# A decoder step: weight sums made by transfers instead of additions, with negations, accumulations and the down products in another order

## The chip, the cores and the metric

The kernel runs on one core of one Trainium2 chip. The metric is device time in microseconds, the median of several runs. All durations below come from one profiled execution of the kernel before.

## The reference

One inference step of a two-layer decoder on 1104 rows (16 meta rows, 1024 prompt rows and 64 sample rows), width 1024, all in float32. Layer 0 mixes by mLSTM, layer 1 by attention with forget gates over a shared K/V and a paged cache. Behind each mixer stands the same feed-forward block:

```python
def swiglu(xn, w_gu, w_d):
    gu = xn @ w_gu
    return (jax.nn.silu(gu[..., :D_FF]) * gu[..., D_FF:]) @ w_d
...
        h = h + swiglu(rmsnorm(h, prm['norm_ffn'][l]), prm['w_gate_up'][l], prm['w_down'][l])
        if l == N_A_LAYERS - 1:
            shared = shared_kv(h, prm['norm_kv'], prm['w_kvf'], prm['b_fg_b'], prm['k_norm_b'])
```

The inner width D_FF is 2816. Outputs are the activations, the mLSTM state, and K, V and forget values.

## The kernel before

**Arithmetic.** A float32 operand is split into a high part (ACT, `whi` L367) and a low part (DVE, `wlo` L368); a product is three matmuls, high by high, high by low and low by high. The 1104 rows stand in three groups of 336, 384 and 384, feature by row.

**Stages, in order of time.** Loading and transposing the input, with the value projection behind it (0 to 133.5 us); query, key and the mLSTM (from 169.5); out projection and the start of the feed-forward block (to about 640); its units of two columns of blocks, some 21 us each (to about 1078); down (to about 1350); K, V and queries of layer 1 (to about 1715); attention; the second feed-forward block (2210 to 2725) and its down product (to 2976).

**Loading, L735 to 777.** Nine row tiles are transposed on PE (`hps`), and ACT and DVE copy each half into `hs` (L761, L764), one of two buffers; POOL makes a low part (`x0l`, L767), then stores `hs` to a DRAM copy of the residual, `hD` (L776).

**Gate/up.** It runs as a scheme of block products with fewer multiplications. POOL makes sums of weight blocks (L135), ACT and DVE split them, PE multiplies (`m`, L1566), DVE forms the results (L1514, L1515). Results go to DRAM tiles `hT` (L1522). Some are also needed negated: `h_minus` negates in place on ACT (L1538) and stores, all that have gathered at the end of every second unit. `ACCUMULATE` lists, unit by unit, sums of one `hT` tile into another by accumulating transfers on POOL's queue (L1543).

**Down.** It is 15 products (`DOWN`), in chains that share an accumulator, four 128-row blocks each; weights and operands are loaded a few steps ahead (`w_load`, `x_load`), split, and multiplied (`dps`, L1978). Accumulators lie in four banks of tag d, and DVE adds a finished chain into the residual `H` (L1960). Two products use a difference of weights, made by `w_sub` on POOL (L1705). Nine other weights are sums of blocks of `w_down`, read from DRAM tiles `wc`: `combine` makes them, in seven pieces per layer, by six loads (L2030), nine additions on DVE (L2035) and nine stores (L2036). Layer 0's pieces stand in the value projection, layer 1's in the projection of K and queries. The norm of the next stage runs on POOL among others (`ns`, L442).

**Order.** In gate/up and down the order of PE, DVE, ACT and POOL is as written (`manual_schedule`, `fixed`); elsewhere a scheduler orders an engine's instructions by their dependencies. Each engine then runs its list strictly in order; POOL's and SP's transfers wait in their engine's list too. POOL's transfers share one software queue; SP's, with the weight loads (L351, L101), a hardware queue.

Of the kernel before, what the change touches and what calls it, by code (L numbers as in the profile page):

```python
# [16 lines left out]
P = 128  # L17
# [41 lines left out]
PAIRS = ((2, 0, 0, 1), (12, 1, 0, 2), (7, 0, 1, 3), (9, 4, 3, 4))  # L59
# [6 lines left out]
LATER = (("s5", "n20"), ("s13", (2, 0)), ("s3", (2, 0)), ("s3", (2, 1)), ("s11", "n21"), ("s11", (2, 2)), ("s9", (2, 2)),  # L66
         ("s6", (2, 2)))
ACCUMULATE = {9: (("s1", (0, 1), 0, 4), ("s1", (0, 1), 4, 7)), 11: (("s5", (0, 2), 0, 4), ("s5", (0, 2), 4, 7)),
# [3 lines left out]
              19: tuple((a, b, 0, 4) for a, b in LATER[:4]), 20: tuple((a, b, 0, 4) for a, b in LATER[4:])}  # L72
DOWN = ((12, 1, ((1, 0, 1), (1, 1, -1)), None, True), (14, 1, ((0, 1, 1),), None, False),
# [203 lines left out]
class Net:  # L277
# [237 lines left out]
    def mlp(self, H, w, l, heads=None, cb=None, early=None):  # L515
# [8 lines left out]
        with self.pool(self.uid("nsp")) as sp, self.pool(self.uid("npp"), bufs=2, space=PSUM) as pn:  # L524
# [28 lines left out]
            with ExitStack() as c:  # L553
# [89 lines left out]
                order.enter_context(self.tc.manual_schedule(engines={E.PE, E.DVE, E.Activation}))  # L643

                rows = (4, 5, 6, 7, 0, 1, 2, 3) if cb else range(KT)
                for x, m in enumerate(rows):
# [14 lines left out]
            with cw if not cb else ExitStack():  # L661
# [8 lines left out]
                if cb:  # L670
# [3 lines left out]
                    self.ffn(H, flat, l, weights, order, mix, each, after, self.first_values, cw, cb, self.first_weights)  # L674
                else:
                    self.ffn(H, flat, l, weights, order, mix, each, None,
# [106 lines left out]
def phase_a(self, vt):  # L783
# [7 lines left out]
    with ExitStack() as c3:  # L791
# [13 lines left out]
        with ExitStack() as cw, self.pool("ppA0", bufs=4, space=PSUM) as pp:  # L805
# [21 lines left out]
            with self.pool("wcA") as wc:  # L827
                for c in range(3):
                    cols, evac = part(c)
                    for j in ((0, 1, 2), (3, 4), (5, 6))[c]:  # L830
                        self.combine(0, j, lambda x: wc.tile([P, 512], F32, name=self.uid("wc"), tag=f"wc{x}",
                                                             bufs=2 if isinstance(x, tuple) else 1))
                    self.tm_proj(cols, None, pp, "mm0", 4, evac, halves=None if c else ahead)
# [2188 lines left out]
```

## Time and profile before

| what | us |
|---|---|
| median of 3 runs (lowest to highest) | 2981.53 (2977.31 to 2983.31) |
| profiled execution | 2987.69 |
| its span | 2986.0 |
| PE busy | 2770.6 |
| DVE busy | 1898.1 |
| ACT busy | 1342.2 |
| POOL busy | 1175.1 |

The mean granted clock of TensorE was 0.973. The hardware queue moved 339.15 MB, the software queue 189.97 MB. Busy time is an average over the stages; a row "A <- B" in a view of waits says that A's engine was idle until B, with the total in us, how often, and the longest. L followed by a number is a line of the kernel before; rows of the changed kernel's order have its own line numbers.

### The profile page before, as it was taken

How to read it: one execution, taken by the hardware profiler on the slowest of the kernel's cores; microseconds unless marked ns; L12 is line 12 of the kernel's file. 1: busy time of each engine (PE TensorE's matmuls, PEld its weight loads, DVE VectorE, ACT ScalarE, POOL GpSimd, SP SyncE). 2: the span in 40 equal slices, each digit the busy share in tenths (PEclk: the TensorE clock that was granted, in tenths of full speed). 3: DMA queues.
4: the chain of work that ended last, by engine and by line, in shares of the span. 5: the costliest groups of instructions: out<-in, count | busy, mean ns of one | idle time of the engine just before them, and what ended most of it. 6: DMA issues, size and time to landing. Idle time of an engine off the chain costs nothing.

```text
span 2986.0 us, 53985 instructions
## 1 busy us (share of the span) xinstructions
PE 2770.6 (93%) x19981; PEld 2629.5 (88%) x19981; DVE 1898.1 (64%) x3781; ACT 1342.2 (45%) x2734; POOL 1175.1 (39%) x1714
## 2 busy tenths in 40 slices
PE   7769999999999889988988999999999999988998
PEld 7768888999999889988988988777899999988997
DVE  6453565787776656773366643577568777765676
ACT  5122354454444334443343444677544444433443
POOL 4522333156565510223476310455315556551031
PEclk9979999999999989998999999999999999999999
DMA  7855656223445699644577486544413344669973
GB/s 226 279 178 144 172 144 193 86 90 124 138 124 139 146 270 316 225 157 131 184 264 270 162 299 247 196 163 141 139 55 93 121 138 124 147 150 285 296 247 141
DMA packets 379683, 533.18 MB, mean 179 GB/s; under 512 B 36046, under 2 KB 282346, under 8 KB 378394
## 3 DMA queue, kind: packets, MB, share of 16 engines
q1 hardware_dynamic: 315730, 339.15, 35.0%
q0 software_dynamic: 62464, 189.97, 22.4%
q8 instruction: 157, 2.57, 0.4%
q14 instruction: 108, 0.88, 0.1%
q10 hardware_dynamic: 1224, 0.60, 0.1%
HBM read 373.32 MB, written 194.83 MB: 190 GB/s over the span
## 4 chain that ended last, share of the span: by engine, by line
PE 29%; DVE 6%; DMA 5%; issue 4%; POOL 4%; ACT 2%; SPq 0%; DVEq 0%; ACTq 0%; POOLq 0%
PE m L1566 8%; PE dps L1978 7%; PE sp L2784 2%; PE op L2880 1%; DMA hT<-Ht 1%; PE bps L293 1%; DVE s L2793 1%; PE tp L2843 1%; PE pops L293 1%; PE pops L294 1%; PE pops L295 1%; DVE slot L368 1%; PE bps L294 1%; PE bps L295 1%; PE ktp L2487 1%
## 5 line engine op out<-in xcount | busy, mean ns | idle before, releaser
L1566 PE MATMUL m<-x1h,slot 128*128 128x384 f32 x640 | 179.4, 339 | 3.8 <-DVE ns L1515 1.5
L368 DVE TENSOR_TENSOR slot<-slot,slot 128x512 fp32r<-128x512 f32 (+3 forms) x175 | 153.4, 878 | 46.2 <-ACT slot L367 39.2
L1978 PE MATMUL dps<-dn0xh,dn0wh 128*128 128x384 f32 (+1 forms) x444 | 152.0, 342 | 21.4 <-DVE vA L1960 14.4
L1566 PE MATMUL m<-x0h,slot 128*128 128x336 f32 x640 | 167.8, 317 | 0.0
L1978 PE MATMUL dps<-dn1xh,dn1wh 128*128 128x384 f32 (+1 forms) x444 | 150.6, 339 | 14.5 <-DVE Ht L1960 10.2
L367 ACT CAST slot<-slot 128x512 fp32r<-128x512 f32 (+3 forms) x175 | 114.3, 655 | 83.8 <-PE m L1566 65.7
L1978 PE MATMUL dps<-dn0xl,dn0wh 128*128 128x384 f32 (+1 forms) x444 | 150.2, 338 | 0.2 <-DVE dn0xl L368 0.2
L1978 PE MATMUL dps<-dn1xl,dn1wh 128*128 128x384 f32 (+1 forms) x444 | 149.7, 337 | 0.5 <-DVE dn1xl L368 0.5
L1978 PE MATMUL dps<-dn0xh,dn0wl 128*128 128x384 f32 (+1 forms) x444 | 150.0, 338 | 0.0
L1978 PE MATMUL dps<-dn1xh,dn1wl 128*128 128x384 f32 (+1 forms) x444 | 149.3, 336 | 0.0
L1566 PE MATMUL m<-x2h,slot 128*128 128x384 f32 x480 | 136.4, 338 | 0.0
L368 DVE TENSOR_TENSOR slot<-Ht,slot 128x256 fp32r<-128x256 f32 (+2 forms) x100 | 81.8, 820 | 78.2 <-ACT slot L367 78.2
L368 DVE TENSOR_TENSOR slot<-vA,slot 128x256 fp32r<-128x256 f32 (+2 forms) x100 | 81.5, 816 | 78.5 <-ACT slot L367 78.5
L135 POOL TENSOR_TENSOR slot<-vA 128x256 f32<-128x256 f32 x80 | 70.4, 889 | 153.2 <-DMA vA<-in_w_gate_up 131.5
L135 POOL TENSOR_TENSOR slot<-Ht 128x256 f32<-128x256 f32 x80 | 69.8, 883 | 153.2 <-DVE T_1l L168 69.8
L1566 PEld LDWEIGHTS m<-x1h,slot 128*128 128x128 f32 x640 | 117.6, 188 | 5.9 <-DVE ns L1515 2.1
L1566 PEld LDWEIGHTS m<-x0h,slot 128*128 128x128 f32 x640 | 113.9, 189 | 0.0
L442 POOL TENSOR_TENSOR ns<-ns,x2l 128x384 f32<-128x384 f32 (+1 forms) x18 | 24.5, 1360 | 225.6 <-ACT x2l L440 225.1
L1566 PE MATMUL m<-T_2h,slot 128*128 128x384 f32 x320 | 99.1, 351 | 13.8 <-ACT ns L1572 8.8
L1978 PEld LDWEIGHTS dps<-dn0xh,dn0wh 128*128 128x128 f32 x444 | 86.5, 195 | 24.7 <-ACT dn0wh L367 11.4
L1566 PE MATMUL m<-x1l,slot 128*128 128x384 f32 x320 | 108.0, 338 | 0.0
L1566 PE MATMUL m<-T_4h,slot 128*128 128x384 f32 x320 | 96.9, 343 | 9.8 <-ACT Ht L1572 4.4
(867 smaller groups left out, 10277.0 us busy)
## 6 DMA issues: line engine op xcount, KB each, us to landing
wraw<-in_w_in_a SPq DMA_DIRECT2D x40, 512.0 KB, 4.1
vA<-in_w_gate_up SPq DMA_DIRECT2D x40, 512.0 KB, 4.0
Ht<-in_w_gate_up SPq DMA_DIRECT2D x40, 512.0 KB, 4.2
kp<-in_cache_k SPq DMA_DIRECT2D x32, 512.0 KB, 6.9
vp<-in_cache_v SPq DMA_DIRECT2D x32, 512.0 KB, 8.4
wc<-wc POOLq DMA_DIRECT2D x63, 256.0 KB, 3.9
wc<-wcv POOLq DMA_DIRECT2D x63, 256.0 KB, 3.2
x2h<-wc SPq DMA_DIRECT2D x30, 512.0 KB, 10.1
```

What stands on the lines that cost most here:

```text
L135: self.net.nc.gpsimd.tensor_tensor(out=o, in0=a, in1=b, op=op)
L293: mm(ps, sh, mh, start=first, stop=False)
L294: mm(ps, sh, ml, start=False, stop=False)
L295: mm(ps, sl, mh, start=False, stop=last)
L367: self.nc.scalar.copy(hi, src)
L368: self.nc.vector.tensor_tensor(out=lo, in0=src, in1=hi.bitcast(F32), op=ALU.subtract)
L1566: nc.tensor.matmul(u.b[b][:, :n], w[p][:, k], x[q][:, k], start=new and k == i == 0, stop=k == 1 and i == 2, skip_group_check=True)
L1978: nc.tensor.matmul(acc[m][:, :c], w[a][:, k, m * P : m * P + P], x[b][:, k, :c], start=lead and k == q == 0, stop=k == len(ts) - 1 and q == 2,
L2487: nc.tensor.transpose(pk[:, j, :], R["kp"][n][:, (4 * g + j) * P : (4 * g + j + 1) * P], self.ident)
L2784: nc.tensor.matmul(ps[z][:, :n], a[r, qs], b[r, at : at + n], start=(y == 0), stop=(y == 2))
L2793: nc.vector.tensor_tensor_reduce(out=ss[z, u][:, at + o : at + e], in0=ps[z][:, o:e], in1=diag[x][:, z] if y else ncb[:, z, at + o : at + ...
L2843: nc.tensor.transpose(pt[:, h, y], ss[z, u][r, j * P : j * P + P], self.ident[r, r])
```

## The change

The sums of blocks of `w_down` are no longer made on DVE. `combine` is a generator of 18 steps per layer: a copy of a block from DRAM to DRAM into `wc`, or an accumulating transfer of a second block onto it, all on POOL's queue. The feed-forward block calls it in steps. Negations are split by quarters of a unit. `ACCUMULATE` and `LATER` are reordered so that consecutive transfers have different targets. The weight difference is made on DVE (`sub`). The chain of products 2, 8, 10, 5 comes first in down; accumulators lie in six banks; loads of the residual move. In layer 0 the down weights lie in the places of the gate/up weights, which stay open for the next stage. POOL joins the hand-written order from the last third of the out projection on.

```diff
-PAIRS = ((2, 0, 0, 1), (12, 1, 0, 2), (7, 0, 1, 3), (9, 4, 3, 4))
+COMBINED = ((2, (0, 0), None), (11, (0, 2), None), (12, (1, 0), None), (2, None, (0, 1)), (7, (0, 1), None),
+            (11, None, (1, 2)), (9, (0, 2), None), (8, 2, None), (12, None, (1, 2)), (13, 11, None), (8, None, (1, 1)),
+            (7, None, (1, 1)), (13, None, (1, 0)), (10, 8, None), (14, 13, None), (9, None, (1, 1)), (10, None, (1, 0)),
+            (14, None, (0, 0)))
...
-ACCUMULATE = {9: (("s1", (0, 1), 0, 4), ("s1", (0, 1), 4, 7)), 11: (("s5", (0, 2), 0, 4), ("s5", (0, 2), 4, 7)),
-              15: (("s8", (1, 0), 0, 4), ("s8", (1, 0), 4, 7), ("s6", (1, 0), 0, 4)),
+ACCUMULATE = {9: (("s1", (0, 1), 0, 4), ("s5", (0, 2), 0, 4)), 11: (("s1", (0, 1), 4, 7), ("s5", (0, 2), 4, 7)),
+              15: (("s8", (1, 0), 0, 4), ("s6", (1, 0), 0, 4), ("s8", (1, 0), 4, 7)),
...
-DOWN = ((12, 1, ((1, 0, 1), (1, 1, -1)), None, True), (14, 1, ((0, 1, 1),), None, False),
+DOWN = ((2, 1, ((0, 0, 1),), None, True), (8, -1, ((0, 2, -1),), None, False), (10, 1, ((1, 2, 1),), None, False),
+        (5, -1, ((1, 0, -1),), (1, 0), False),
+        (12, 1, ((1, 0, 1), (1, 1, -1)), None, True), (14, 1, ((0, 1, 1),), None, False),
         (1, -1, ((0, 0, -1),), (0, 0), False),
-        (2, 1, ((0, 0, 1),), None, True), (8, -1, ((0, 2, -1),), None, False), (10, 1, ((1, 2, 1),), None, False),
-        (5, -1, ((1, 0, -1),), (1, 0), False),
...
+                comb = self.combine(l)
...
+                    if x in (1, 5):
+                        next(comb)
...
-                    self.combine(0, j, lambda x: wc.tile([P, 512], F32, name=self.uid("wc"), tag=f"wc{x}",
...
-        def h_minus():
-            while negs:
-                o, x, j = negs.pop(0)
+        def h_minus(cs):
+            for y in [y for y in negs if y[0] in cs]:
+                negs.remove(y)
+                _, o, x, j = y
...
-                nc.gpsimd.tensor_tensor(out=a, in0=a, in1=b, op=ALU.subtract)
+                sub(a, a, b)
...
-                        if x % 2 == 0:
-                            h_minus()
+                    if x % 2 == 0 and g != 2:
+                        h_minus((("s1", "v2"), ("t4", "c15"), (), ("s2", "e"))[g])
+                    if g == 3:
+                        next(comb, None)
...
-            cw.close()
+            if not early:
+                cw.close()
...
+            if early:
+                view = lambda y: self.slots[y][:, : KT * P].rearrange("p (k n) -> p k n", k=2)
+                for x in range(2):
+                    got["raw", x] = view(x)
+                for x, y in ((0, 0), (1, 1), (2, 2), (4, 3)):
+                    got["wh", x], got["wl", x] = view(2 + y), view(LOW[y])
...
-                        acc[m] = bank("dps", "d")
+                        acc[m] = bank("dps", "f" if banks in (4, 5) or early and banks % 6 > 3 else "d")
+                        banks += 1
...
-                if 4 <= i < 12:
-                    h_add(*LATER[i - 4], 4, 7)
+                if i in (1, *range(4, 18, 2)):
+                    h_add(*LATER[i // 2 - (i > 1)], 4, 7)
...
+def combine(self, l):
+
+    e, w = self.nc.gpsimd, self.I["w_down"][l]
+    half = lambda z, k: w[7 * k * P : 7 * k * P + 7 * P, 512 * z : 512 * z + 512]
+    comb = self.comb[l] = {}
+    for p, a, b in COMBINED:
+        if a is not None:
+            comb[p] = self.dram.tile([7 * P, 512], F32, name=f"wc{l}_{p}")
+            e.dma_start(comb[p], half(*a) if isinstance(a, tuple) else comb[a])
+        else:
+            e.dma_start(comb[p], half(*b), accum_op=ALU.add)
+        yield
```

What this does to the lists of the engines is seen at three places. The first is POOL at the start of the program, in the loading of the input (`wc0_` and `wc1_` are the combined weights of layer 0 and 1; DMASW are the marks that earlier transfers of POOL's queue have landed). Before:

```order
L776 DMA hD_90<-hs_156 1024x1x80 [waits DVE_49,Activation_49]
L767 TENSOR_TENSOR x0l_3_146<-xy_223,x0h_2_145 128x4x128 [waits Activation_49]
L776 DMA hD_90<-hs_203 1024x1x128 [waits DVE_49]
L767 TENSOR_TENSOR x0l_3_146<-xy_284,x0h_2_145 128x4x128 [waits Activation_49]
L776 DMA hD_90<-hs_258 1024x1x128 [waits DVE_49]
```

And now:

```order
L2047 DMA wc0_12_6018<-in_w_down 896x512
L2047 DMA wc1_2_23912<-in_w_down 896x512
L2049 DMA wc0_2_5645<-in_w_down 896x512 [waits DMASW0_49]
L2047 DMA wc0_7_6162<-in_w_down 896x512
L782 DMA hD_90<-hs_156 1024x1x80 [waits DVE_49,Activation_49]
L2047 DMA wc1_11_24053<-in_w_down 896x512
L2047 DMA wc1_12_24284<-in_w_down 896x512
L2049 DMA wc1_2_23912<-in_w_down 896x512 [waits DMASW3_49,DMASW1_49]
L2047 DMA wc1_7_24428<-in_w_down 896x512 [waits DMASW2_49]
L773 TENSOR_TENSOR x0l_3_146<-xy_223,x0h_2_145 128x4x128 [waits Activation_49]
L782 DMA hD_90<-hs_203 1024x1x128 [waits DVE_49]
L773 TENSOR_TENSOR x0l_3_146<-xy_284,x0h_2_145 128x4x128 [waits Activation_49]
```

Two more copies, of `wc0_2` and `wc0_11`, stand a few rows earlier. The first five steps of both layers, ten transfers, now stand ahead of the second store of `hs`; no step of layer 0's feed-forward block or layer 1's holds them back. ACT's copies into `hs`, in the changed kernel, wait for the store two tiles earlier, through DMASW6 for the first store and DMASW3 for the second:

```order
L767 COPY hs<-hps_259 128x512 [waits DMASW6_49]
L771 CAST x0h_145<-xy 128x4x128 [waits DVE_49]
L817 COPY vA_101<-tmps_298 80x2x128 [waits PE_49]
L819 COPY gates<-tmps_298 80x16
L731 COPY rb<-rps_325 128x128 [waits PE_49]
L714 ACTIVATE vA_103,r_344<-xin 128x8x128 [waits DMAHW4_49]
L716 ACTIVATE r_344<-r_344,eps 128x1 [waits Activation_49]
L766 CAST x1h_329<-xy 128x4x128 [waits DVE_49]
L767 COPY hs<-hps_332 128x512 [waits DMASW3_49]
```

ACT's list itself has not moved here. The second place is SP, with the weight loads of query and key (`wraw`, 128x8x128). Before, they come after the loads of the cache's forget values and wait for transfers of POOL's queue, the stores of `combine`:

```order
L957 DMA lp<-in_cache_logf 128x16 [waits DMAHW5_49]
L351 DMA wraw_2233<-in_w_in_a 128x8x128 [waits DMASW5_49,DMASW4_49,DMASW6_49,DMASW3_49,DMASW7_49,DMASW0_49,DMAHW6_49,DVE_49,PE_49]
L351 DMA wraw_2310<-in_w_in_a 128x8x128 [waits DMASW6_49,DMASW2_49,DMAHW7_49,DMASW1_49,DMASW0_49]
L351 DMA wraw_2420<-in_w_in_a 128x8x128 [waits DMAHW6_49,DMAHW0_49,DVE_49]
L351 DMA wraw_2482<-in_w_in_a 128x8x128 [waits DMAHW7_49,DMAHW1_49,DVE_49]
```

And now:

```order
L354 DMA wraw_1264<-in_w_in_a 128x4x256 [waits DMAHW6_49,DMAHW4_49,DVE_49]
L354 DMA wraw_1996<-in_w_in_a 128x8x128 [waits DMAHW5_49,DMAHW2_49,PE_49]
L354 DMA wraw_1270<-in_w_in_a 128x4x256 [waits DMAHW0_49,DVE_49]
L354 DMA wraw_2073<-in_w_in_a 128x8x128 [waits DMAHW7_49,DMAHW1_49]
L354 DMA wraw_2183<-in_w_in_a 128x8x128 [waits DMAHW5_49,DVE_49]
```

They stand ahead of the forget values, between the last loads of the value projection, and wait for no transfer of POOL's queue. The third place is POOL in a late unit of layer 0's gate/up, with the accumulating transfers. Before:

```order
L1543 DMA hT_480_6101<-hT_487_6108 128x1344 [waits DMAHW6_49,DMAHW7_49,DMAHW5_49,DMASW0_49]
L1543 DMA hT_472_6093<-hT_477_6098 128x4x336 [waits DMAHW4_49,DMASW1_49]
L1543 DMA hT_473_6094<-hT_477_6098 128x4x336
L1543 DMA hT_473_6094<-hT_474_6095 128x1536 [waits DMAHW7_49,DMAHW1_49,DMASW2_49]
L135 TENSOR_TENSOR slot_5147<-vA_102 128x256 [waits DMAHW4_49,Pool_49]
```

And now:

```order
L1546 DMA hT_428_5872<-hT_431_5875 128x1344 [waits DMAHW6_49,DMAHW7_49,DMAHW5_49,DMASW6_49]
L1546 DMA hT_424_5868<-hT_419_5863 128x4x336 [waits DMAHW4_49,DMASW7_49]
L1546 DMA hT_423_5867<-hT_419_5863 128x4x336
L1546 DMA hT_427_5871<-hT_432_5876 128x1536 [waits DMAHW2_49,DMAHW1_49,DMASW1_49]
L138 TENSOR_TENSOR slot_4910<-vA_102 128x256 [waits DMAHW4_49,Pool_49]
```

Before, the fourth transfer adds into the tile that the third has just been given, and waits for it, with the weight sums (`slot`) behind; now its target is another. The negations of L1538 stand at the same places of ACT's list as before.

More of the change, by code (lines that the diff above doesn't have):

```diff
@@ L642, in mlp @@
                 fixed.close()
-                order.enter_context(self.tc.manual_schedule(engines={E.PE, E.DVE, E.Activation}))
+                order.enter_context(self.tc.manual_schedule(engines={E.PE, E.DVE, E.Activation, E.Pool}))
+                comb = self.combine(l)
                 rows = (4, 5, 6, 7, 0, 1, 2, 3) if cb else range(KT)
@@ L826, in phase_a @@
                     self.tm_proj(cols, None, pp, "mm0", 4, evac, halves=held, only=i)
[L827 to L830, printed above, removed]
-                        self.combine(0, j, lambda x: wc.tile([P, 512], F32, name=self.uid("wc"), tag=f"wc{x}",
-                                                             bufs=2 if isinstance(x, tuple) else 1))
-                    self.tm_proj(cols, None, pp, "mm0", 4, evac, halves=None if c else ahead)
+            for c in range(3):
+                cols, evac = part(c)
+                self.tm_proj(cols, None, pp, "mm0", 4, evac, halves=None if c else ahead)
         pp = c3.enter_context(self.pool("ppA", bufs=2, space=PSUM))
@@ L1484, in ffn @@
 @_add(Net)
-def ffn(self, H, flat, l, weights, order, mix, each, after, end, cw, cb=None, early=None):
+def ffn(self, H, flat, l, weights, order, mix, comb, each, after, end, cw, early=None):
     nc, I = self.nc, self.I
@@ L1792, in ffn @@
         ends = direct(1, 0)
+        next(comb)
         for i, k in enumerate(ks):
@@ L1804, in ffn @@
         ends = direct(0, 1)
+        next(comb)
         m.cast(2, pure(0))
@@ L1835, in ffn @@
         ends = direct(1, 1)
+        next(comb)
         weights.split(2, 0)
@@ L1914, in ffn @@
             self.sq = lambda x: x2[1].bitcast(F32)[:, x % 2 * SL : x % 2 * SL + SL]
-            ring = {"n": list(place["raw"]), "v": list(place["tmp"][:3])}
+            ring = {"n": place["raw"][:3], "v": place["tmp"][:3]}
+            if early:
+                ring = {"n": [got["raw", 2], got["tmp", 0]], "v": [got["tmp", 1], got["tmp", 2]]}
             def ny(nm):
@@ L2253, in then @@
                     behind.append(lambda: turn(q, v4))
-                if 4 * gi + c < 7:
-                    wide = [fp.tile([P, NT, 256], F32, name=self.uid("wcv"), tag="vst").rearrange("p i d -> p (i d)")
-                            for _ in range(2)]
-                    places = [y[:, z * 512 : z * 512 + 512] for y in wide for z in range(4)]
-                    self.combine(1, 4 * gi + c, lambda x: places.pop())
                 self.tm_proj([w[:, 256 * c : 256 * c + 256]], g, pp, "b", 4, evac, then)
```

51 lines of the change are left out of this document (18 added, 33 removed), and 4 rows, old and new, of the table ACCUMULATE.

## Prediction

> **What bounds the kernel now.** I read the page's first part, then PE's waits, then windows. In the page's totals:
>
> ```profile
> span 2986.0 us, 53985 instructions
> PE 2770.6 (93%) x19981; PEld 2629.5 (88%) x19981; DVE 1898.1 (64%) x3781; ACT 1342.2 (45%) x2734; POOL 1175.1 (39%) x1714
> ```
>
> TensorE bounds it, and the change neither adds nor removes a matmul. What can move is the 215 us in which PE is idle, and its clock after a gap. PE's waits name the holes:
>
> ```profile
> PE mmA L293 <- ACT whi L367: 35.8, 1, 35.8
> PE btp L2222 <- DVE raw L2249: 22.6, 11, 4.2
> PE dps L1978 <- DVE vA L1960: 14.4, 5, 6.7
> PE m L1566 <- ACT ns L1572: 10.6, 13, 2.4
> PE dps L1978 <- DVE Ht L1960: 10.2, 2, 5.9
> PE tmps L293 <- ACT slot L361: 7.6, 1, 7.6
> ```
>
> The largest is one wait of 35.8 us. The windows show each place (columns: window, length, then busy us and count for PE, PEld, DVE, ACT, POOL; clock, DMA share, GB/s):
>
> ```profile
> 10.00:20.00 10.00, 3.71 (x14) 2.38 (x15) 7.70 (x24) 7.39 (x15) 2.90 (x3) 1.00 1.08 373
> 60.00:133.50 73.50, 73.50 (x642) 73.37 (x640) 34.26 (x49) 13.89 (x32) 40.04 (x74) 1.00 0.85 278
> 133.50:169.50 36.00, 0.16 (x2) 0.05 (x1) 13.58 (x21) 1.72 (x3) 19.62 (x37) 0.54 0.78 265
> 650.00:800.00 150.00, 148.07 (x862) 146.34 (x863) 116.83 (x185) 72.95 (x152) 92.04 (x92) 1.00 0.35 108
> 834.00:860.00 26.00, 24.82 (x144) 24.13 (x144) 20.37 (x35) 11.72 (x26) 15.49 (x15) 1.00 0.70 182
> 1015.00:1050.00 35.00, 28.26 (x133) 26.43 (x132) 19.98 (x31) 9.83 (x22) 17.43 (x18) 0.85 0.75 149
> 1276.00:1292.00 16.00, 9.27 (x40) 8.91 (x39) 15.18 (x18) 5.92 (x9) 5.66 (x2) 0.79 0.79 275
> 1450.00:1500.00 50.00, 48.56 (x425) 48.24 (x424) 19.47 (x39) 17.44 (x46) 20.33 (x35) 1.00 0.59 199
> 1500.00:1650.00 150.00, 129.55 (x1058) 127.60 (x1057) 98.70 (x190) 55.74 (x158) 105.23 (x173) 0.95 0.80 275
> 2700.00:2750.00 50.00, 39.54 (x211) 38.60 (x211) 31.42 (x48) 19.25 (x28) 9.99 (x14) 0.90 0.93 304
> 2850.00:2900.00 50.00, 50.00 (x301) 49.87 (x301) 38.15 (x51) 22.44 (x33) 13.49 (x7) 1.00 0.76 261
> 2900.00:2950.00 50.00, 44.04 (x235) 43.04 (x234) 40.61 (x50) 19.70 (x28) 13.08 (x5) 0.90 0.61 211
> ```
>
> A stage's undisturbed rate comes from its best row: 862/150 = 5.75 matmuls per us in gate/up, 301/50 = 6.02 in down, 425/50 = 8.5 in the k/q projection. Missing matmuls over that rate are lost time.
>
> **Part 1, the start.** PE is full from 60 to 133.5, then stands until 169.5, because the query/key weights come late. SP says why, and ACT what it waits for:
>
> ```profile
> SPq L351 <- DMA wc<-wc: 50.1, 4, 22.9
> ACT whi L367 <- DMA wraw<-in_w_in_a: 44.4, 5, 34.1
> ```
>
> The weight load reuses memory of the combining, so it queues behind its last stores. In the changed order those loads stand before the log-forget loads and wait for no transfer of POOL's queue: the 36 us hole goes, if nothing else comes. But something does. The new order puts the first five transfers of both layers, eight copies and two accumulates of 896x512 floats (1.835 MB each), at the head of POOL's queue, ahead of hD<-hs. There are two hs buffers; ACT's copy into hs of row tile 2 waits for the first hD store to land, that of tile 3 for the second, and the second stands behind all ten. ACT runs in order, so everything for tiles 3 to 8 stands behind that copy. In the timeline before:
>
> ```profile
> 7.28 0.18 POOL L1016 TENSOR_SCALAR_AFFINE_SELECT bm<-bm 64x8 f32<-64x8 f32 x1
> 28.57 0.58 ACT L761 COPY hs<-hps 128x512 f32<-128x512 f32 x1
> 55.20 1.62 POOL L767 TENSOR_TENSOR x2l<-xy,x2h 128x512 fp32r<-128x512 f32 x1 [3.12 <-ACT x2h L765]
> ```
>
> From tile 3's copy to the last low half is 56.8 − 28.6 = 28.2 us, and from there to the end of the value projection 133.5 − 56.8 = 76.7 us of full PE. So query/key now starts at D + 28.2 + 76.7, where D is when the second hD store lands, or when it did before if D is early; before, at 169.5.
>
> D needs the price of the transfers. An accumulate has a row, in the window where one pair of hT sums ran, and the hardware loads of the first 60 us have another:
>
> ```profile
> q0 software_dynamic: 928, 1.20, 28.4%
> ...
> q1 hardware_dynamic: 6018, 8.26, 43.8%
> ```
>
> 28.4% of 26 us is 7.4 us of all 16 engines for 1.20 MB, so 1.835 MB takes 11.3 us. A DRAM-to-DRAM copy has no row: from below, the load rate at 10 to 20 us, 373 GB/s, gives 4.9 us; from above, the accumulate, which reads two operands, gives 11.3. I take 8, the middle, since a copy does more than a load and less than an accumulate. Half of the 8.26 MB of loads falls before D and shares the engines, 11 us, and the two hD stores (0.85 MB) take 2.3. Issue starts near 8 us (POOL's setup ends at 7.5). D = 8 + 8·8 + 2·11.3 + 13.3 = 108, query/key starts at 213: **+43 us**. With copies at 4.9 D is 83, +19; with accumulates at that rate also, D is 70, +6; with copies at 11.3, D is 134, +70. So the ends are +6 and +70.
>
> The Trainium skill, "DMA: Bandwidth & Descriptors", section "Latency and other measured facts", gives 214 GB/s as the full rate of copies between HBM tensors; by it a copy is estimated at 8.6 us and the sum would be −8 instead of −13. Its section "Issuing engines are not separate DMA queues" says that transfers issued from any engine run on the same 16 engines and interleave; by that the weight loads would suffer too, as counted here; the DMA share of 1.08 at 10 to 20 us agrees that there is no spare.
>
> **Part 2, combining leaves the k/q projection.** DVE's 63 additions per layer sit in its queue ahead of the normalisation that PE waits for:
>
> ```profile
> L2035 DVE TENSOR_TENSOR wc<-wc,wc 128x512 f32<-128x512 f32 x63 | 42.8, 691 | 54.4 <-DMA wc<-in_w_down 38.6 <-DMA wc<-wc 14.8
> ```
>
> Each is 0.69 us plus waits for its load. From 1500 to 1650 PE does 1058 matmuls against 8.5·150 = 1275: 25.5 us lost, of which the btp wait (22.6) is most. I take **−22**, bounds −10 (ACT or POOL, at 37% and 70% of that window, holds next) and −25.5.
>
> **Part 3, shared weight places.** The kvf loads no longer wait for a place of their own and stand eight rows earlier in SP's order: the 7.6 us slot wait shrinks, **−7**, bounds 0 and −10.
>
> **Part 4, what gate/up pays.** Thirteen transfers per layer are left, five copies and eight accumulates, 5·8 + 8·11.3 = 130 us of all engines, one per unit of about 21 us, over about 240 us. At 650 to 800 the DMA share is 0.35, so it becomes near 0.9. The weight loads' landing:
>
> ```profile
> vA<-in_w_gate_up SPq DMA_DIRECT2D x40, 512.0 KB, 4.0
> ...
> vA<-in_w_gate_up SPq DMA_DIRECT2D x3, 512.0 KB, 5.1
> ```
>
> 4.0 us over all, 5.1 in the window with accumulates, where PE lost only 26 − 144/5.75 = 1 us. The step is issued behind POOL's sums, when the next load goes out too, so they meet; the sums have some slack before the split. I take 1 us per accumulate step, **+16** for both layers; bounds 0 (slack covers it) and +70 (each of 26 steps delays a unit by 2.7 us). POOL's own issue, 1 to 2 us, hides in its waits for loads.
>
> **Part 5, same-target sums apart.**
>
> ```profile
> POOL hT L1543 <- DMA hT<-hT: 74.1, 7, 13.6
> POOL ns L442 <- ACT x2l L440: 225.1, 10, 56.8
> ```
>
> POOL stood 74 us for these; behind it stand the next unit's weight sums, then the split, then PE. From 1015 to 1050 PE made 133 of 201 matmuls: 11.8 us lost, with a clock of 0.85. ACT's negations wait there too (below), and stay. I take 8 of the 11.8 per layer: **−16**, bounds 0 and −24.
>
> ```profile
> ACT Ht L1538 <- DMA hT<-Ht: 36.3, 16, 5.0
> ACT vA L1538 <- DMA hT<-vA: 35.6, 15, 5.7
> ```
>
> The change splits the negations by quarter, but in ACT's order they stand where they stood before. I cost that edit at nothing; these 72 us of ACT waits, and what PE loses by them, remain.
>
> **Part 6, down.** The weight subtraction moves from POOL to DVE. It stood behind POOL's norm sums, which wait for ACT (the 225 us above):
>
> ```profile
> 2899.95 3.68 POOL L442 TENSOR_TENSOR ns<-ns,x2l 128x384 f32<-128x384 f32 x2
> 2903.59 3.39 POOL L1705 TENSOR_TENSOR x2h<-x2h,dn1raw 128x1024 f32<-128x1024 f32 x1
> ```
>
> PE loses (301 − 235)/6.02 = 11.0 us from 2900 to 2950, and at 1276 to 1292 (96 − 40)/6.02 = 9.3 us in layer 0. On DVE (81% busy in the late window) the 128x1024 operation costs 1 to 2 us, in reach of the row of 0.69 for 128x512; I count it inside the gain. Six accumulator banks shorten the waits for DVE's evictions (14.4 and 10.2 us) in part: 6 us in layer 0, 1 to 4 in layer 1, where the stage's start (2700 to 2750: 90 missing matmuls, 15 us) is bound by transfers at a share of 0.93 and stays. **−15** and **−12**; bounds −5 and −24, −3 and −25.
>
> **Sum.** 43 − 22 − 7 + 16 − 16 − 15 − 12 = −13 us. The profiled execution took 2987.69 us (1.7 around its span) and would take 2974.7; the runs' median is 2981.53, so I predict **2968 us**.
>
> **Rivals.** (a) *The hoisted transfers cost more* (slower): copies at the accumulate's rate. Place: the second hD store; price +70 instead of +43; sum +14, 2995 us. It decides from copies of 9.6 us on (13/8 over 8). For it: the start is full of loads, share 1.08; against: a copy reads one operand. 0.22. (b) *Gate/up starves* (slower): loads and steps start together and POOL's sums come late; 3 us per accumulate step are +48 instead of +16, 3000 us. For it: a share near 0.9; against: 1 us lost in 834 to 860. 0.14. (c) *The start is nearly hidden* (faster): all ten at the load rate, +6 instead of +43: 2931 us. For it: a copy's price may be a load's; against: the accumulate's row, and the loads already there. 0.20. (d) *It doesn't do what it says*: no pacing at the start, the negations unmoved, and if the reorderings merely move waits elsewhere, the 43 us of parts 5 and 6 shrink to 30: no change, 2981 us. 0.14. My forecast has 0.30.
>
> **Range and chances.** 0.2% (6 us) is about what a measurement of this kernel can tell from no change. Faster: forecast and (c), 0.50; same: (d), 0.14; slower: (a) and (b), 0.36. The likeliest case's own range is 2950 to 2975. All good ends together, 6 − 25.5 − 10 + 0 − 24 − 24 − 25 = −102.5, give 2879, which is not met at once; (c) with a little more of these is 2925. Upward, (a) and (b) together, 27 + 32 on 2968, give 3027.
>
> **What would show it.** Right: no wait of PE for whi near 133, but PE, ACT and POOL idle from about 25 to 108 us, ending with an hD store's landing, and query/key starting near 213; btp's wait for raw gone; no hT-to-hT wait on POOL around 1020 to 1050; norm sums no longer ahead of a weight subtraction. Wrong: query/key starting before 190 or after 235; weight loads in gate/up landing above 8 us and PE below 5.5 matmuls per us there; or in down new waits for transfers in place of those removed.

## The result and the profile after

The changed kernel takes 3045.18 us (median of 4 runs, 3042.38 to 3047.64) against 2979.49 us of the kernel before on the same chip: a ratio of 1.0219, 95% interval 1.0201 to 1.0236. It is 66 us slower where I forecast 13 us faster, outside my range of 2950 to 2975 us and beyond its far end of 3027. The page of the changed kernel:

```profile
span 3045.9 us, 53528 instructions
PE 2778.2 (91%) x19981; PEld 2632.6 (86%) x19981; DVE 1820.2 (60%) x3671; ACT 1341.2 (44%) x2734; POOL 1041.7 (34%) x1526
```

DVE and POOL have lost 78 and 133 us of work, and PE is about as busy as before. As the run is slower, that work did not bound it. PE's waits, the costliest:

```profile
PE hps L750 <- ACT hs L767: 51.1, 4, 28.6
PE m L1569 <- ACT Ht L1575: 20.7, 11, 5.4
PE m L1569 <- ACT fs L1575: 18.5, 8, 7.1
PE dps L2001 <- DVE vA L1982: 15.5, 4, 6.3
PE m L1569 <- ACT vA L1575: 15.2, 8, 5.0
```

The wait of 35.8 us for the query/key weights is gone and so is btp's for raw; a wait for ACT's copy into hs stands in their place, and gate/up (m, now L1569) waits longer for ACT's bank copies (the copies of results out of the accumulators): before, its four rows were 10.6, 9.4, 8.0 and 6.6 us.

Both kernels do the same matmuls in the same order, except inside down and for four small ones ahead of query/key, so the start of the same matmul in two traces shows how long each stage took. Five later kernels are in the same table (us). Each column is cut at the same matmuls, some of them a few us inside a stage: query/key's first matmul itself starts at 169.5 us before and at 195.9 after.

| stage | before | after | held | old comb. | moved | spread | attention |
|---|---|---|---|---|---|---|---|
| start to query/key | 173.1 | 198.1 | 134.7 | 175.0 | 136.6 | 136.3 | 137.1 |
| query/key, mLSTM | 323.6 | 318.5 | 321.2 | 320.4 | 354.9 | 319.5 | 318.7 |
| out projection, start of feed-forward | 153.9 | 154.3 | 167.9 | 155.2 | 155.6 | 165.2 | 161.3 |
| gate/up, layer 0 | 432.4 | 464.8 | 467.7 | 432.5 | 435.2 | 449.2 | 437.0 |
| down, layer 0 | 253.2 | 252.8 | 253.4 | 251.8 | 250.2 | 251.2 | 250.8 |
| transition, V | 139.2 | 125.9 | 125.9 | 125.9 | 127.0 | 133.9 | 132.6 |
| K and queries | 238.5 | 207.8 | 207.5 | 238.2 | 243.3 | 210.8 | 210.8 |
| sample attention, entry to prompt | 185.4 | 195.6 | 195.9 | 195.0 | 209.2 | 185.5 | 184.8 |
| prompt attention | 246.8 | 249.3 | 249.5 | 249.5 | 246.8 | 248.4 | 261.7 |
| out projection, layer 1 | 116.1 | 116.1 | 128.0 | 116.1 | 116.6 | 127.6 | 121.0 |
| gate/up, layer 1 | 455.2 | 493.8 | 492.6 | 456.8 | 458.7 | 460.3 | 457.7 |
| down, layer 1, end | 261.7 | 262.2 | 262.1 | 262.1 | 262.0 | 262.8 | 261.7 |

After against before: +25.0 at the start, −5.1, +0.4, **+32.4**, −0.4, −13.3, **−30.7**, +10.2, +2.5, 0, **+38.6**, +0.5: together +60, as the spans (3045.9 − 2986.0) say. The chain at the start is the one I had drawn. ACT stands idle until the stores of hs have landed, and its copies for row tiles 2 and 3 begin only at 65.8 and 92.3 us:

```profile
ACT hs L767 <- DMA hD<-hs: 48.9, 2, 25.9
```

```profile
65.75 0.59 ACT L767 COPY hs<-hps 128x512 f32<-128x512 f32 x1 [25.87 <-DMA hD<-hs]
92.28 0.59 ACT L767 COPY hs<-hps 128x512 f32<-128x512 f32 x1 [23.03 <-DMA hD<-hs]
```

In windows (the same columns as in the prediction) PE is nearly empty until then, with all transfer engines busy, and later full with the engines idle:

```profile
25.00:60.00 35.00, 4.62 (x19) 3.66 (x17) 4.14 (x13) 4.65 (x9) 5.52 (x6) 0.56 1.05 323
60.00:85.00 25.00, 5.78 (x33) 5.55 (x33) 3.75 (x12) 3.46 (x9) 2.09 (x2) 0.64 1.06 286
140.00:196.00 56.00, 56.00 (x491) 56.00 (x490) 2.45 (x2) 9.47 (x22) 0.00 (x0) 1.00 0.05 6
```

What the software queue and the loads moved in the first 100 us of the changed kernel (packets, MB, share of 16 engines):

```profile
q0 software_dynamic: 6097, 20.39, 68.1%
q1 hardware_dynamic: 4962, 7.21, 22.2%
```

The transfers themselves, in the page's list of issues of the changed kernel (KB each, median us to landing), with the weight loads of gate/up, whose medians were 4.0 and 4.2 us before:

```profile
wc<-in_w_down POOLq DMA_DIRECT2D x28, 1792.0 KB, 15.5
...
vA<-in_w_gate_up SPq DMA_DIRECT2D x40, 512.0 KB, 6.1
Ht<-in_w_gate_up SPq DMA_DIRECT2D x40, 512.0 KB, 5.1
...
wc<-wc POOLq DMA_DIRECT2D x8, 1792.0 KB, 7.9
```

Two of these medians need care. That of `wc<-in_w_down` mixes the ten transfers at the start, which queue one behind another, with those in gate/up. And the trace gives a landing for only 6 of the 40 vA loads and 14 of the 40 Ht loads: of the six, three land after 3.9 to 4.3 us, as before, and three after 7.9 to 10.0.

A copy from scratch to scratch lands after 7.9 us, which is 232 GB/s for 1.835 MB. The Trainium skill's figure for copies between HBM tensors ("DMA: Bandwidth & Descriptors", section "Latency and other measured facts", 214 GB/s at full rate, there with padded rows and on other queues) nearly agrees.

### The profile page after: what moved, and what is told of

Read it like the earlier page. It is cut to its first block, busy times and chain, and to the rows that moved or that the text cites. A ratio compares the mean times of both kernels' runs of the same rounds, so it can differ in the third digit from the quotient of the medians.

```text
span 3045.9 us, 53528 instructions
## 1 busy us (share of the span) xinstructions
PE 2778.2 (91%) x19981; PEld 2632.6 (86%) x19981; DVE 1820.2 (60%) x3671; ACT 1341.2 (44%) x2734; POOL 1041.7 (34%) x1526
## 5 line engine op out<-in xcount | busy, mean ns | idle before, releaser
L371 DVE TENSOR_TENSOR slot<-slot,slot 128x256 fp32r<-128x256 f32 (+2 forms) x193 | 176.6, 916 | 60.6 <-ACT slot L370 56.6
L2001 PE MATMUL dps<-dn0xh,slot 128*128 128x384 f32 (+1 forms) x704 | 187.4, 344 | 19.6 <-DVE vA L1982 15.5
L1569 PE MATMUL m<-x1h,slot 128*128 128x384 f32 x640 | 182.9, 343 | 18.3 <-DVE Ht L1516 6.5
L370 ACT CAST slot<-slot 128x256 fp32r<-128x256 f32 (+2 forms) x193 | 130.9, 681 | 94.8 <-PE m L1569 71.6
L1569 PE MATMUL m<-x0h,slot 128*128 128x336 f32 x640 | 168.4, 318 | 0.0
L2001 PEld LDWEIGHTS dps<-dn0xh,slot 128*128 128x128 f32 x704 | 132.0, 195 | 22.3 <-issue 14.0
L138 POOL TENSOR_TENSOR slot<-vA 128x256 f32<-128x256 f32 x80 | 74.1, 937 | 207.3 <-DMA vA<-in_w_gate_up 127.0
L1569 PEld LDWEIGHTS m<-x1h,slot 128*128 128x128 f32 x640 | 119.0, 190 | 22.4 <-DVE Ht L1516 7.1
L1569 PE MATMUL m<-T_4h,slot 128*128 128x384 f32 x320 | 100.9, 356 | 40.2 <-ACT Ht L1575 16.5
L1569 PE MATMUL m<-x2h,slot 128*128 128x384 f32 x480 | 135.8, 337 | 0.0
L2001 PE MATMUL dps<-dn0xl,slot 128*128 128x384 f32 (+1 forms) x352 | 120.6, 343 | 0.5 <-DVE dn0xl L371 0.5
L1569 PEld LDWEIGHTS m<-x0h,slot 128*128 128x128 f32 x640 | 114.4, 189 | 0.0
L1569 PE MATMUL m<-T_2h,slot 128*128 128x384 f32 x320 | 98.3, 348 | 15.9 <-ACT ns L1575 13.7
L1569 PE MATMUL m<-x1l,slot 128*128 128x384 f32 x320 | 108.9, 340 | 0.0
L1569 PEld LDWEIGHTS m<-T_4h,slot 128*128 128x128 f32 x320 | 61.1, 194 | 48.8 <-ACT Ht L1575 18.5
```

Source lines behind the costliest of these rows:

```text
L138: self.net.nc.gpsimd.tensor_tensor(out=o, in0=a, in1=b, op=op)
L370: self.nc.scalar.copy(hi, src)
L371: self.nc.vector.tensor_tensor(out=lo, in0=src, in1=hi.bitcast(F32), op=ALU.subtract)
L1569: nc.tensor.matmul(u.b[b][:, :n], w[p][:, k], x[q][:, k], start=new and k == i == 0, stop=k == 1 and i == 2, skip_group_check=True)
L2001: nc.tensor.matmul(acc[m][:, :c], w[a][:, k, m * P : m * P + P], x[b][:, k, :c], start=lead and k == q == 0, stop=k == len(ts) - 1 and q == 2,
```

## The experiments

**Held: the first five transfers of a layer kept at their written place.** They stood at the head of a hand-written order of POOL with no instruction and no data ahead of them; a small sum that reads the residual now stands there.

```diff
...
                     unit(2, m, x)
+                    if x == 0:
+                        nc.gpsimd.tensor_tensor(out=held, in0=H[2][:, m, :8], in1=H[2][:, m, 8:16], op=ALU.add)
```

> The changed kernel with one small addition on POOL, a sum of 8 columns of the residual, ahead of the first transfer of the combining in each layer, so that the first five transfers of a layer cannot run before the last third of its out projection. Theory A (the ten hoisted transfers hold the second store of the residual and with it ACT): the value projection ends near 133 us instead of 196, the 36 us wait for the query/key weights stays away, so query/key starts near 134; 56 us less than the changed kernel, about 2989 us, and up to 10 us more if the five transfers now disturb the out projection. Rival B (the input loads are slow for another reason, the order of the other loads): value projection still ends after 170 us, 3030 us or more.

3004.17 us (ratio to before 1.0067, interval 1.0041 to 1.0094), 41 us less than the changed kernel. Query/key starts at 134.7 us, 63 us earlier than in the changed kernel and 38 earlier than in the kernel before: theory A stands. What was too small is the price of five transfers at once beside the out projections: 13.6 us in layer 0 and 11.9 in layer 1, where up to 10 in all had been expected.

**Negations left out.**

```diff
-                nc.scalar.activation(o, o, AF.Copy, scale=-1.0)
                 h_put(o, x, j)
```

> The changed kernel without the negations: ACT no longer negates in place after the store, the positive values are stored twice, so that four of the stored operands have the wrong sign; everything else, the transfers of the combining too, is as in the changed kernel. Theory N (the transfers of the combining slow the stores of gate/up results, ACT waits for these landings before it negates, and the bank copies behind it keep PE waiting): the 32 us and 40 us which gate/up lost in layer 0 and 1 against the kernel before go, and some 20 us more of the waits that were there before; about 2960 to 2975 us. Rival L (the weight loads come late because they share the engines with the transfers): at most 15 us are gained, 3030 us.

3022.52 us (1.0141, 1.0114 to 1.0168), 23 us less: between the two. The stages decide. Gate/up takes 453.2 us in layer 0 and 482.0 in layer 1: 11.6 and 11.8 less than the changed kernel, but 20.8 and 26.8 more than the kernel before. Whether those 12 us per layer belong to the transfers, the same edit on the kernel before tells.

**Negations left out of the kernel before.** The edit is the same one.

> The kernel before without the negations (the positive values are stored twice, so four of the stored operands have the wrong sign); same-target sums in their old order. Theory N2 (PE's losses near the late units, 1015 to 1050 us and the like, come from ACT that waits for a store's landing before it negates in place, and not from POOL that waits for a same-target sum): gate/up becomes 10 to 20 us shorter in each layer though POOL's waits of 13 us stay; 2945 to 2965 us. Rival (my prediction's step, POOL's late weight sums): at most 3 us per layer, 2975 us or more.

2958.75 us (0.9928, 0.9899 to 0.9956), the time that theory N2 expects. Gate/up takes 420.8 and 445.2 us, 11.6 and 10.0 less than before. So the negations cost about 11 us per layer with and without the transfers, and the transfers cost 32.4 (453.2 − 420.8) and 36.8 us (482.0 − 445.2) without the negations, against 32.4 and 38.6 with them: theory N is out. The window that I had read as a loss by same-target sums, 1015 to 1050 us, in this kernel, first the window, then POOL's wait in it, with one wait longer than the one before:

```profile
1015.00:1050.00 35.00, 28.19 (x149) 27.55 (x148) 18.00 (x27) 11.37 (x25) 15.15 (x18) 0.90 0.72 150
...
POOL hT L1542 <- DMA hT<-hT: 21.6, 2, 14.9
```

The same wait before:

```profile
POOL hT L1543 <- DMA hT<-hT: 13.2, 1, 13.2
```

The stage as a whole is 11.6 us shorter with POOL waiting 21.6 us. The 149 matmuls, instead of 133, are not the same ones, since the program is 12 us further by then. By the starts of the same matmuls, those that took before 34.9 us, from 1015 to 1050, take 32.2 here: less than 3 of the 11.6 us come back in that window, the rest in other units. So theory N2 has the price of the negations right, but they explain only a small part of what PE loses in this window.

**The combining of the kernel before, all other edits kept.**

```diff
-                comb = self.combine(l)
+                comb = iter(())
...
+            with self.pool("wcA") as wc:
...
+                        self.combine(0, j, lambda x: wc.tile([P, 512], F32, name=self.uid("wc"), tag=f"wc{x}",
...
```

> The changed kernel with the combining of the kernel before (loads, additions on DVE and stores in the value projection and in the k/q projection) and all other edits. If the edits on same-target sums, down order, banks and the weight difference gain what I costed (16, 15, 12, and 7 for the shared places): about 2930 us. If they gain next to nothing, as the aligned traces of before and after suggest (gate/up in layer 0 from its unit 9 on 1 to 3 us less, down 0 and 0, the transition 14 less, attention 10 more): about 2973 us. In both cases the 36 us wait for the query/key weights is back and gate/up shows no loss.

2984.01 us (1.0005, 0.9994 to 1.0016): the other edits together gain nothing that can be measured, worse than either number. Gate/up and down are within 2 us of before, the transition is 13.3 us shorter, the entry to prompt attention about 10 us longer. So the 66 us, as a net sum of losses and gains, come with the combining by transfers. And the same-target wait: here POOL has none in that window, its sums begin at 1018 instead of 1033, and PE makes 144 matmuls instead of 133, but is later by 4 us at 1040 and level at 1050; ACT waits for the landings as before (before: `10.3, 3, 5.1`). The window, and ACT's wait in it:

```profile
1015.00:1050.00 35.00, 29.16 (x144) 28.08 (x143) 21.32 (x33) 10.71 (x24) 21.64 (x22) 0.85 0.81 171
...
ACT vA L1545 <- DMA hT<-vA: 11.2, 3, 5.0
```

**Accumulates replaced by copies.**

```diff
-            e.dma_start(comb[p], half(*b), accum_op=ALU.add)
+            e.dma_start(comb[p], half(*b))
```

> The changed kernel with each of the 18 accumulating transfers replaced by a plain copy of the same block onto the same place, so that the combined weights are wrong; as many transfers of the same size in the same order. Theory P (an accumulate holds the engines about twice as long as a copy, and that is what makes weight loads late): the start is 10 to 15 us shorter, the loss in gate/up falls by half or more, about 3000 us. Rival Q (the count of the transfers and their bytes decide, or their place in POOL's order): 3030 to 3045 us.

2973.16 us (0.9966, 0.9954 to 0.9977), 72 us less than the changed kernel, more than theory P had expected. Gate/up falls from 464.8 to 438.8 and from 493.8 to 463.0 us, of 32.4 and 38.6 lost 26.0 and 30.8 come back. In the start only 5.2 us do: two accumulates there are dearer than two copies by 2.6 us each. In this kernel's list of issues:

```profile
wc<-in_w_down POOLq DMA_DIRECT2D x28, 1792.0 KB, 10.1
...
vA<-in_w_gate_up SPq DMA_DIRECT2D x40, 512.0 KB, 4.2
```

In gate/up of layer 0 alone, where each goes by itself, POOL's queue (packets, MB, share of 16 engines) and its seven accumulates, in the changed kernel from 700 to 1110 us:

```profile
q0 software_dynamic: 12896, 32.30, 41.5%
...
wc<-in_w_down POOLq DMA_DIRECT2D x7, 1792.0 KB, 15.0
```

and the seven copies in their place in this kernel, from 690 to 1090 us:

```profile
q0 software_dynamic: 9968, 33.38, 34.9%
...
wc<-in_w_down POOLq DMA_DIRECT2D x7, 1792.0 KB, 9.4
```

An accumulate lands after 15.0 us and a copy after 9.4. The queue held the engines 170 us (41.5% of 410) instead of 140 (34.9% of 400), some 4.4 us more per accumulate. The few landings that the trace gives of the weight loads (6 of 40) have a median of 4.2 us with copies, 4.0 before and 6.1 with accumulates. Who waits for those loads are POOL's weight sums, here in layer 0's gate/up of this kernel:

```profile
POOL slot L138 <- DMA vA<-in_w_gate_up: 71.5, 11, 10.4
```

of the changed kernel:

```profile
POOL slot L138 <- DMA vA<-in_w_gate_up: 127.0, 14, 14.1
```

and of the kernel before:

```profile
POOL slot L135 <- DMA vA<-in_w_gate_up: 58.5, 12, 10.5
```

**The transfers moved out of gate/up**, into the value projection, query/key and output gates (layer 0) and the projection of K and queries (layer 1), each behind a small sum on POOL that reads a fresh result.

```diff
+def paced(self, l, at):
...
+    with self.tc.manual_schedule(engines={mybir.EngineType.Pool}):
+        self.nc.gpsimd.tensor_tensor(out=self.held, in0=at[:, :8], in1=at[:, 8:16], op=ALU.add)
+        next(comb, None)
```

> The changed kernel with the 18 transfers of the combining taken out of gate/up and spread one by one over other stages, each held back by a small sum on POOL that reads a result just made: layer 0's 7 over the value projection, 6 over query/key, 5 over the output gates; layer 1's 18 over the projection of K and queries, one for every fourth row tile. Theory A+L (the loss is where the transfers stand: ahead of the residual's stores at the start, and beside the weight loads of gate/up): from the aligned traces, the start 40 us less than before, the transition and k/q 13 and 31 less, attention 13 more, gate/up as in the kernel before, so about 2905 us, and up to 20 more if the transfers disturb their new neighbours. Rival M (such transfers slow whatever runs beside them, since the engines' time is the same everywhere): k/q and query/key lose what gate/up gains, above 2960 us.

3005.45 us (1.0079, 1.0055 to 1.0103): a miss of 100 us. The start and gate/up are as theory A+L says (136.6; 435.2 and 458.7), but query/key with the mLSTM takes 354.9 us, 36 more than in the changed kernel, K and queries 243.3, 35 more, sample attention 14 more. The seven in the value projection cost next to nothing: 136.6 against 134.7. PE's waits in this kernel from 130 to 500 us, for a load of what was stored on POOL's queue, and for the store's buffer, and the one in K and queries over the run:

```profile
PE sps L1280 <- DMA qk<-qkD: 12.5, 2, 10.5
PE mmA L296 <- ACT stg L878: 11.4, 2, 7.7
...
PE btp L2264 <- DVE raw L2291: 18.9, 7, 6.0
```

So rival M is right where the neighbours use POOL's own queue: the transfers into and out of qkD land after 6.4 us there (median, longest 16.6) instead of 4.5 (longest 8.8) in the changed kernel. Whether they are late by the queue's order or by the engines' time was not tried apart.

**The slot counter begun at 0** (on the moved kernel).

```diff
-                self.slot = 1
+                self.slot = 0
```

> The kernel with the transfers moved (first of this batch), and the counter of shared weight places begun at 0 instead of 1 after layer 0's down, so that SP's loads for prompt attention wait for the same transfers as in the kernel before and not for PE's last gate product. Theory S (the 11 us lost at the entry to prompt attention come from this place): 10 us less than the moved kernel, the entry takes 14 us and not 25. Rival: the transition loses its 13 us gain in exchange, no difference.

2999.36 us (1.0065, 1.0045 to 1.0085). The entry to prompt attention (80 matmuls at its start) falls from 24.7 to 13.9 us as theory S says, and the transition with V grows from 127.0 to 132.8, so about half of what the entry gains is lost there, where the rival expected all of it. The 6 us less in the medians is within what the intervals leave open; the stage times are plain. In the changed kernel SP's first load for prompt attention waits for PE's last gate product, with the other loads behind it, where the kernel before had four of them out at 1868 us:

```profile
SPq L2707 <- PE bps L298: 15.4, 1, 15.4
```

The counter decides which shared place the last weights lie in, and those places become the attention's.

**The weight difference back on POOL** (on the moved kernel).

```diff
-                sub(a, a, b)
+                nc.gpsimd.tensor_tensor(out=a, in0=a, in1=b, op=ALU.subtract)
```

> The kernel with the transfers moved (first of this batch), with the weight difference in down back on POOL. Theory D (the difference was late on POOL and is as late on DVE, whose splits and additions fill it at that point): down in both layers within 4 us of the moved kernel. Rival, my prediction's step (POOL's queue behind the norm sums costs 9 and 11 us): 15 to 20 us more than the moved kernel.

3007.4 us (1.0086, 1.0065 to 1.0108). Down takes 254.1 us instead of 250.2 in layer 0, and 265.0 instead of 262.0 with the end in layer 1: theory D, within 4 us; the move is worth 3 to 4 us per layer, not 9 to 11.

**Spread: placed where nobody waits.** Layer 0: 8 in the value projection, 5 in the out projection and the start of feed-forward, 5 in single units of gate/up; layer 1: 3 in V, 10 in prompt attention, 5 in the out projection; counter at 0.

```diff
...
+                    if groups.index((hp, g)) in (2, 5, 8, 11, 14, 17, 20, 23, 26, 29):
+                        self.step(1)
```

> The changed kernel with the 18 transfers per layer placed where the traces of the runs so far show neither loads that PE waits for nor traffic on POOL's queue that others wait for: layer 0's 8 over the value projection, 5 over the out projection and the start of feed-forward, 5 in every second or third unit of gate/up; layer 1's 3 in the value projection of K/V, 10 in prompt attention (one for every third group), 5 in its out projection; the slot counter as in the kernel with that one edit. Theory L (an accumulate is dear only beside a stream that somebody waits for): the start is 40 us shorter than in the kernel before, query/key as before, k/q 31 shorter, gate/up of layer 0 at most 12 longer, attention at most 10 longer: 2910 to 2940 us. Rival M (such transfers disturb whatever runs beside them): attention and the out projection lose 30 us or more, 2965 us or above.

2957.79 us (0.9921, 0.9899 to 0.9944): faster than both kernels, by less than theory L expected. Prompt attention takes its ten for nothing (248.4 against 249.3). The out projections lose 10.9 and 11.5 us, gate/up of layer 0 16.8 us for five steps. The out projection's wait in this kernel:

```profile
PE ghps L1488 <- DVE ogc L1490: 8.7, 1, 8.7
```

**All of layer 1 in prompt attention**, with the steps in another order, so that the value projection takes four of the accumulates.

```diff
...
+                    if groups.index((hp, g)) in (1, 3, 4, 6, 8, 10, 11, 13, 15, 16, 18, 20, 21, 23, 25, 27, 28, 30):
+                        self.step(1)
```

> The last placement with all 18 transfers of layer 1 in prompt attention, where 10 of them cost nothing, none in the K/V value projection and the out projection, and the steps of a layer in another order, so that layer 0's value projection takes four accumulates and four copies. Theory L: the out projection of layer 1 gives back its 11 us, gate/up of layer 0 3 to 6 us with fewer accumulates left, attention stays within 10 us: 2940 to 2950 us. Rival M (18 are too many for attention: its loads of keys and rows for the next heads come late): attention 20 us or more longer, 2965 us or above.

2944.38 us (0.9875, 0.9854 to 0.9896): the fastest of all, 39 us less than the kernel before on the same chip and about 100 less than the changed one. Gate/up of layer 0 gives back 12 us, but not by fewer accumulates, as expected: three accumulates and two copies stand there in both kernels, in another order, and the last two a unit earlier here. The out projection of layer 1 gives back 7; 5 of its loss stay, though no transfer stands there any more. Neither was followed up. Eighteen steps cost prompt attention 13 us, more than the 10 expected. PE there now waits for POOL, and POOL for a load of attention's own, which the ten steps of the kernel above did not delay:

```profile
PE tp L2915 <- POOL rx L2908: 10.7, 3, 4.9
```

```profile
POOL nd L2802 <- DMA ncb<-cD: 9.0, 2, 8.7
```

## Why the prediction was wrong

**Part 1, the start: mechanism right, size off.** The copies into hs, the second store behind ten transfers, the vanished hole: each is in the trace. D was sized at 108 us and the copy for tile 3 began at 92; the start costs +25.0 instead of +43. The term that was mis-sized is the price of the transfers. In the run with copies for accumulates the software queue's 20.90 MB of the first 100 us held the engines 61.1 us, which is about 5.4 us per copy where I had put 8; in the changed kernel 20.39 MB took 68.1 us, so an accumulate held them about 4 us longer, some 9.6 us where I had put 11.3. The loads went the other way: 22 us where I had put 11.

**Part 4, what gate/up pays: the step that failed.** I took 1 us per accumulate step from a window in which PE lost 1 us beside a pair of hT sums, 1.2 MB. Measured are +32.4 and +38.6 us, 71 instead of 16, or 4.4 us per accumulate step, just past its bound of 70. Rival (b) had the place right, late weight loads through shared engines, and priced it at 48. The runs show that the loss is the transfers': by the starts of the same matmuls it grows in layer 0 from nothing to 33.6 us while they go out, until about 932 us of the changed kernel, and not afterwards. Four fifths of it are the accumulates' own (26.0 and 30.8 us return with copies of the same size), 3.3 and 3.9 us on average for each beyond a copy's price, and POOL's sums then wait 127 us for the loads instead of 58.5 in layer 0. The engines were not as full there as I had summed: their share from 671 to 938 us, while the transfers went out, is 0.76, where I wrote near 0.9. Nor could the landings I compared carry the choice: 4.0 us rests on 6 of the 40 loads, and 5.1 on one of three. Why PE lost only 1 us beside the hT sums stays open. How the loads' lateness reaches PE I argue from the rows: POOL, then ACT's and DVE's splits, then ACT's bank copies; no run isolates it. The Trainium skill's sentence that transfers from any engine interleave on the same 16 engines ("DMA: Bandwidth & Descriptors", section "Issuing engines are not separate DMA queues") agrees with this, and so would have spoken for rival (b).

**Part 5, same-target sums: false.** The step "behind it stand the next unit's weight sums, then the split, then PE" did not hold. With POOL's wait gone (the old combining) gate/up is unchanged, and with POOL's wait longer (before without negations) it is 11.6 us shorter. ACT's wait for a landing before it negates in place, which I quoted and took as staying, costs PE more than POOL's wait; but it does not explain the window either. The 236 matmuls around it take 53.4 us before, 53.1 with the sums in the new order (the old combining), 50.0 without negations, and 47.8 with the new order and no negations (the changed kernel without negations). At the stage's best rate, 5.75 per us, they would take 41. What holds PE there for more than half of the lost time stays open.

**Part 6, down: false.** The weight difference, no longer behind POOL's norm sums, is now behind DVE's splits; ACT waits for DVE instead. The 18 us around the same place (DVE's is the third busy time of a window), and what ACT waits for, first before (ACT's row from 2660 to 2990 us), then after:

```profile
2898.00:2916.00 18.00, 13.71 (x79) 13.42 (x78) 17.71 (x14) 6.74 (x10) 14.30 (x6) 0.96 0.67 221
...
ACT dn1wh L367 <- POOL x2h L1705: 9.3, 4, 5.6
```

```profile
2960.00:2978.00 18.00, 14.41 (x81) 13.48 (x80) 17.28 (x21) 8.11 (x12) 3.28 (x2) 1.00 0.76 259
...
ACT dn1wh L370 <- DVE x2h L1517: 5.6, 2, 4.4
```

DVE was full in that stretch already, 17.7 of 18 us; I had read DVE's 81% over 50 us and not these 18. Whatever the six banks gain in layer 0, down as a whole is 0.4 us shorter there. One loss that stands against it lies at 1180 to 1193 us of the changed kernel, where its first chain is evicted (added to the residual): PE waits for DVE's eviction, DVE for ACT, ACT for an operand that is loaded while sums into hT still run:

```profile
PE dps L2001 <- DVE vA L1982: 6.3, 1, 6.3
...
ACT dn0xh L1744 <- DMA dn0tmp<-hT: 16.0, 2, 8.3
...
POOL hT L1546 <- DMA hT<-hT: 11.0, 2, 8.3
```

**Parts 2 and 3: right in kind.** K and queries gain 30.7 us against 22, more than my bound of 25.5; the transition gains 13.3 against 7, more than its bound of 10 as well. What I did not see is the other end of the shared places, +10.2 us at the entry to prompt attention.

**The sum.** Predicted 43 − 22 − 7 + 16 − 16 − 15 − 12; measured +25 − 31 − 13 + 71 + 0 + 0 + 0, and +10 at the entry, +2.5 in prompt attention and −5 in query/key, which I did not follow up. Two errors add up: a cost on a stage that PE bounds was taken at its light end, and three gains were booked from the engine that waited longest, not from what PE waited for. The start, smaller than forecast by 18 us, and the larger gains of parts 2 and 3 made the miss smaller; that was luck.

## What to carry to other kernels

Here a transfer without operands to wait for came to stand at the head of its queue's order, however late it was written, and a small sum that reads fresh data held it back: tie such a transfer to data. Work that is moved from an engine to the transfer queues was cheap here only in some stages, so place it stage by stage (the value projection took eight transfers and prompt attention ten at next to no cost; gate/up, query/key, K and queries and the out projections did not). And before a wait is booked as a gain, look at which engine PE itself waits for in that window, and how full the engine is that takes over the work.

## What was not expected of the hardware

An accumulating transfer was clearly dearer than a copy, and what that cost the kernel depended on what stood beside it. In layer 0's gate/up an accumulate of 1.835 MB landed after 15.0 us and a copy in its place after 9.4, and it held the engines some 4.4 us longer. Eight of them per layer cost that stage 26 and 31 us more than copies did. At the start, where ten transfers queue one behind another, two accumulates cost 5.2 us more than two copies. The price is not fixed either: three of them and two copies cost that stage 16.8 us in one placement and 4.6 in another. In prompt attention ten transfers, six of them accumulates, cost nothing that the stage times show (248.4 us with them, 249.3 without).
